# Splitting the loads of a SwiGLU kernel over two issuing queues

## Chip, cores, metric

One core of one Trainium2 chip. The engines go by their short names in the profile: ACT is ScalarE, DVE is VectorE, POOL is GpSimd and SP is SyncE; SP here only issues transfers. The metric is the device time of one execution in microseconds (us). All kernels here move the same data unless it is said otherwise. On one core a run counts as slow when it is over 1.5% above the fastest of its kernel.

## The reference

```python
x = np.random.randn(8192, 8192).astype(np.float32)

def reference(x):
    a, b = np.split(x, 2, axis=-1)
    return a * (b / (1 + np.exp(-b)))      # a * silu(b)
```

268 MB are read, 134 MB written, and there is little arithmetic per byte.

## The kernel before

Each of 32 tiles holds 256 rows of x, two per partition: a load of 8.39 MB and a store of 4.19 MB. Three buffers take turns. Silu runs in place on ACT, the multiply on DVE, and the product is stored from the same buffer, so load i+3 has to wait until store i has landed.

```python
R, BUFS = 2, 3                     # rows per partition, buffers

def load(i, rows=None):            # ... tile i is allocated at its first load
    nc.sync.dma_start(out=tiles[i][:, lo * M : hi * M], in_=xv[...])

def swiglu(i, k, c0=0, cw=half):   # row k of tile i
    nc.scalar.activation(out=b, in_=b, func=_SILU)
    nc.vector.tensor_mul(out=..., in0=a, in1=b)

def store(i, c0=0, cw=R * half):
    (nc.gpsimd if i < last - 1 else nc.sync).dma_start(out=ov[...], in_=tiles[i][...])

for i in range(BUFS):
    load(i)
for i in range(last):
    for k in range(R):
        swiglu(i, k)
    if i == last - 1:
        swiglu(last, 0)
    store(i)
    nxt = i + BUFS
    if nxt < last:
        load(nxt)
    elif nxt == last:
        load(last, (0, 1))
        load(last, (1, 2))
# ... the last tile is stored in two halves
```

## Time and profile before

| | before |
|---|---|
| time, median | 936.34 us (935.99 to 936.64, 3 runs) |
| DVE / ACT busy | 30% / 25% of the span |
| bytes moved | 402.68 MB, mean 431 GB/s over the span |
| ACT waits for loads | 687.3 us, 33 times |
| SP waits for stores | 869.5 us, 29 times |

### The profile page before, as it was taken

How to read it: one execution, taken by the hardware profiler on the slowest of the kernel's cores; microseconds unless marked ns; L12 is line 12 of the kernel's file. 1: busy time of each engine (PE TensorE's matmuls, PEld its weight loads, DVE VectorE, ACT ScalarE, POOL GpSimd, SP SyncE). 2: the span in 40 equal slices, each digit the busy share in tenths (PEclk: the TensorE clock that was granted, in tenths of full speed). 3: DMA queues.
4: the chain of work that ended last, by engine and by line, in shares of the span. 5: the costliest groups of instructions: out<-in, count | busy, mean ns of one | idle time of the engine just before them, and what ended most of it. 6: DMA issues, size and time to landing. Idle time of an engine off the chain costs nothing.

```text
span 934.3 us, 400 instructions
## 1 busy us (share of the span) xinstructions
DVE 283.3 (30%) x65; ACT 229.4 (25%) x66; POOL 16.3 (2%) x34
## 2 busy tenths in 40 slices
DVE  0333312333113332133321333213333133331252
ACT  0323330233311333113331133311333203332041
POOL 0000000000000000000000000000000000000000
DMA  9999999999999999999999999999999999999998
GB/s 404 404 449 426 425 448 424 436 429 446 428 422 441 432 446 424 446 415 453 428 421 456 415 452 421 427 450 415 442 428 441 429 435 428 438 450 414 437 432 383
DMA packets 9507, 402.68 MB, mean 431 GB/s; under 512 B 1056, under 2 KB 1056, under 8 KB 1056
## 3 DMA queue, kind: packets, MB, share of 16 engines
q1 hardware_dynamic: 5184, 276.83, 68.6%
q0 software_dynamic: 4320, 125.83, 31.2%
q14 instruction: 3, 0.02, 0.0%
HBM read 268.44 MB, written 134.22 MB: 431 GB/s over the span
## 4 chain that ended last, share of the span: by engine, by line
DMA 84%; DVE 10%; ACT 4%; issue 1%; DVEq 0%; SPq 0%; ACTq 0%
DMA out_dram<-xt 43%; DMA xt<-in_x_dram 40%; DVE xt L51 10%; ACT xt L50 4%; DVEq L106 0%; SPq L43 0%; ACTq L50 0%; DVEq L51 0%
## 5 line engine op out<-in xcount | busy, mean ns | idle before, releaser
L51 DVE TENSOR_TENSOR xt<-xt 128x4096 f32<-128x4096 f32 (+1 forms) x65 | 283.3, 4359 | 636.9 <-ACT xt L50 633.7
L50 ACT ACTIVATE xt<-xt 128x4096 f32<-128x4096 f32 (+1 forms) x65 | 228.1, 3556 | 687.3 <-DMA xt<-in_x_dram 687.3
L58 POOL DMA_DIRECT2D out_dram<-xt x30 | 16.1, 537 | 854.8 <-DVE xt L51 854.8
L50 ACT ACT_TABLE_LOAD x1 | 1.3, 1283 | 0.7 <-PEq L95 0.7
L95 POOL MEMSET const-float32-0.0<- 128x1 f32 x1 | 0.1, 99 | 0.2 <-issue 0.2
L95 POOL MEMSET const-bfloat16-1.0<- 128x1 bf16 x1 | 0.1, 102 | 0.0
L95 POOL MEMSET const-float32-1.0<- 128x1 f32 x1 | 0.1, 99 | 0.0
L95 POOL MEMSET const-uint8-127<- 128x1 uint8 x1 | 0.1, 99 | 0.0
## 6 DMA issues: line engine op xcount, KB each, us to landing
out_dram<-xt POOLq DMA_DIRECT2D x30, 4096.0 KB, 40.5
xt<-in_x_dram SPq DMA_DIRECT2D x2, 4096.0 KB, 26.4
out_dram<-xt SPq DMA_DIRECT2D x1, 4096.0 KB, 23.8
out_dram<-xt SPq DMA_DIRECT2D x2, 2048.0 KB, 14.5
xt<-in_x_dram SPq DMA_DIRECT2D x31, 33.5
```

What stands on the lines that cost most here:

```text
L50: nc.scalar.activation(out=b, in_=b, func=_SILU)
L51: nc.vector.tensor_mul(out=xt[:, k * half + c0 : k * half + c0 + cw], in0=xt[:, k * M + c0 : k * M + c0 + cw], in1=b,)
L58: (nc.gpsimd if i < last - 1 else nc.sync).dma_start(out=ov[i * P : (i + 1) * P, c0 : c0 + cw], in_=tiles[i][:, c0 : c0 + cw])
L95: nc = _bacc.Bacc("TRN2", target_bir_lowering=False, num_devices=1)
```

## The change

Its intent is to spread the issuing of loads over two queues, so that consecutive loads do not stand behind each other on SP. Stores stay as they were.

```diff
-        nc.sync.dma_start(
+        (nc.sync if i % 2 else nc.scalar).dma_start(
             out=tiles[i][:, lo * M : hi * M], in_=xv[...]
```

ACT executes its instructions in order. A load on ACT that waits for a store therefore also holds back every silu written behind it; the trace of the changed kernel below shows it, 39 us at a time.

## The prediction

> **What bounds the kernel now.** I read the page from the top: first the busy shares and the 40 slices, then the DMA queues, then the chain that ended last, and after that the list of waits and busy times of chosen stretches.
>
> ```profile
> DVE 283.3 (30%) x65; ACT 229.4 (25%) x66; POOL 16.3 (2%) x34
> ...
> DMA  9999999999999999999999999999999999999998
> ...
> q1 hardware_dynamic: 5184, 276.83, 68.6%
> q0 software_dynamic: 4320, 125.83, 31.2%
> ```
>
> The 16 DMA engines are 90% busy or more in 39 slices of 40, and the two queue rows' shares sum to 99.8% of the span. DVE and ACT work less than a third of it. So bytes bound the kernel: 402.65 MB, at this rate:
>
> ```profile
> 287.00:374.00 87.00, 26.55 (x7) 21.37 (x6) 1.60 (x3) 1.00 1.00 434
> 374.00:461.00 87.00, 26.42 (x7) 21.37 (x6) 1.60 (x3) 1.00 1.00 434
> ```
>
> These are stretches of three tiles in the steady part; the last number is GB/s. One tile is an 8.39 MB load and a 4.19 MB store, 12.58 MB, which at 434 GB/s is 29.0 us. The chain confirms it:
>
> ```profile
> 232.52 40.54 DMA out_dram<-xt
> 273.05 0.02 SPq L43
> 273.07 0.03 issue
> 273.11 33.40 DMA xt<-in_x_dram
> 306.50 0.02 issue
> 306.53 0.04 ACTq L50
> 306.56 0.04 issue
> 306.61 3.62 ACT xt L50
> ...
> 319.51 40.49 DMA out_dram<-xt
> ```
>
> Columns: start, length, what. From one store issue to that of three tiles later it is 319.51 - 232.52 = 87.0 us, 29.0 per tile. The chain looks like latency (store lands, then load, silu, multiply, store again), but with three buffers it is the queueing that fills it. A store takes 40.5 us to land although its bytes alone would need 4.19/434 = 9.7 us.
>
> From the same chain I take how two active queues share. Stores are issued 29.0 us apart and take 40.5, so each waits 11.5 us behind its predecessor and is then served for 29.0 us: 4.19/29.0 = 145 GB/s, one third. Loads take 33.5, of which 4.5 behind the predecessor, and 29.0 of service: 8.39/29.0 = 289 GB/s, two thirds. A load packet is a 64 KB row (8.39 MB over 16 engines and 8 rows each) and a store packet a 32 KB row, so one packet in turn from each queue gives just 2:1. Neither queue is ever empty. That is all that the DMA needs.
>
> **What the Trainium skill says.** (1) "DMA: Bandwidth & Descriptors", section "Queues, rings and completion order": each DMA engine goes round-robin between the queue rows that have work, a packet at a time. The 2:1 shares above agree. (2) Same page, "Issuing engines are not separate DMA queues": DMAs from scalar, sync and gpsimd run on the same 16 engines and interleave; another issuer saves only sequencer time. Here that time is small: a load's issue takes 0.328 us in the trace, and SP's wait before it is for the store, not for the sequencer. (3) Same page, "Where 436 GB/s comes from": a 435 GB/s ceiling. The measured 434 is practically at it, so nothing is left to win in the steady part. (4) Same page, "Anatomy of one DMA": a semaphore wait happens on the issuing sequencer before dispatch, and some 2.0 us per DMA are fixed. For the first the wait list below is the case's own sign (on SP). For the second, the first load is issued at 0.74 and its first packets fall into the slice 1.75 to 2.00, so 1.05 us to the first byte; the last packets start in the slice 932.0 to 932.5 and the last store lands at 920.2 + 12.9 = 933.1, about 1 us to the receipt. I take L = 2.1 us from a transfer's last byte to the first byte of the one that waited for it.
>
> ```profile
> SPq L43 <- DMA out_dram<-xt: 869.5, 29, 67.9
> ...
> ACT xt L50 <- DMA xt<-in_x_dram: 687.3, 33, 22.4
> ```
>
> **The change part by part.** Sixteen whole loads (even tiles) move from SP to ACT; SP keeps 15 whole ones and the two halves of tile 31. Bytes, transfers, packets, stores and arithmetic stay. The instruction order of the changed kernel shows on ACT: loads 0 and 2, then four silus, then one load and four silus over and over. Of ACT's loads, 14 wait for a store: load i+3 (i odd) waits for store i, and the silus of tiles i+1 and i+2 stand behind it.
>
> *Issue time:* 16 x 0.328 = 5.2 us of ACT, an engine that is idle 700 us. Off the path.
>
> *Start:* loads 0 and 1 now run side by side and both land at about 2 x 8.39/434 + 2 = 41 us, where load 0 alone landed at 22.7. Store 0 is issued near 41 + 3.6 + 2 x 4.45 = 54 instead of 35.6. But load 2 fills the DMA until then. The bytes flow on; no direct cost.
>
> *Steady state, a pair of tiles:* put store i (odd) landing at t = 0, with load i+2 (on SP) not yet finished, as the walk itself yields below.
> - t = 0: load i+3 is issued on ACT, silus of i+1 start at last (before, they ran some 25 us earlier, as soon as their tile had landed), multiplies end at about 12.6, and store i+1 is issued there. Silus of i+2 follow, store i+2 at about 22.
> - Until 13.7 only loads flow: 13.7 x 434 = 5.9 MB, of which about 1.8 finish load i+2 and 4.1 go to load i+3. Its other 4.3 MB at 289 take 14.8 us, to 28.5. Store i+1 has by then 14.8 x 145 = 2.1 MB and needs 2.05 more alone, 4.7 us: last byte at 33.2.
> - Load i+4 (SP) can flow L later, at 35.3. In these 2.1 us store i+2, already queued, has the DMA to itself: 0.9 MB. Its remaining 3.3 MB go at 145 GB/s and take 22.7 us, to 58.0. Load i+4 has by then 22.7 x 289 = 6.56 MB, and 1.83 MB are left, 4.2 us alone.
> - Store i+2 lands 1 us later: the next t = 0, with the load still in flight, as assumed. The pair took about 58 to 59 us, and twice 29.0 is 58.0.
>
> So the new wait of ACT costs nothing directly: the load left over (2L = 4.2 us of data) covers the L = 2.1 us which the next ACT load needs to start. Before, the silu could run while the store was still in flight, and other transfers covered it; now another order of transfers covers it, but with a cover of only 4.2 - 2.1 = 2.1 us, under one 64 KB packet of an engine (65.5 KB / 27.1 = 2.4 us). That is the weak point.
>
> *Mix:* per pair there are now about 14 + 7 = 21 us in which only loads or only stores flow; before there were none but at start and end. The first 2 to 35 us (loads alone) show 421 and 914 to 930 (stores alone) 421 as well, where mixed stretches show 434, so up to 3% less. Bytes are counted in lumps of 64 KB, and loads 1 and 2 landing 22 us apart speak for less loss, so I take half: 21 x 1.5% = 0.3 us per pair, 15 pairs: 5 us.
>
> ```profile
> 2.00:35.00 33.00, 8.53 (x2) 7.14 (x3) 0.00 (x0) 1.00 0.98 421
> ...
> 914.00:930.00 16.00, 4.49 (x2) 3.44 (x2) 0.00 (x0) 1.00 0.98 421
> ```
>
> *End:* load 30 is ACT's last; silus of 30 and 31 stand behind no more loads. Load 31, then stores 30 and 31, stay FIFO on SP as before, with the same stores-only tail of some 19 us. No change.
>
> Sum: 936 + 0 + 0 + 5 + 0 = 941 us.
>
> **The rivals.** *A. The new wait on ACT stalls the DMA.* For it: ACT is held until a store has landed, silus and stores bunch in pairs, and the cover is 2.1 us. If the 16 engines are apart by a packet or so, some run dry before each ACT load. A gap of 1 us per pair is 15 us (951), one of 2 us 30 us (966). Against it: the cover grows with the same delay L that has to be covered, only the slowest engine counts, and that one always has its backlog. *B. The full round trip is exposed*, with the silu, two multiplies and a store in series after the wait: 15 pairs x 12.6 = 189 us, near 1125. Against it: load i+3 itself, 19.3 us of data, is issued ahead of the silus and fills that time. *C. Two load queues are faster.* For it: the changed ring pattern, and the mostly idle ACT. Against it: 434 of 435 GB/s and 99.8% busy; the floor of the bytes is 402.65/435 = 925.6 us plus about 3 at the ends, 929, which is 0.8% below 936. It can't reach 2%. *D. Nothing at all:* no mix loss and no gap, 936.
>
> **Range and chances.** The middle lies between D and a small share of A. Downwards there is the floor of 929 and no reason to approach it: 934. Upwards, the whole 3% mix loss (10 us) and 0.6 us of gap per pair (9 us) give 955: 956. More than 2% slower begins at 955; I give that 13%, faster by 2% 1%.
>
> **What would show it right or wrong.** Right: the DMA row stays at 9 throughout; ACT's largest wait becomes a store landing ahead of its own loads, about 15 times at some 30 us; silus come in bursts of four every 58 us; loads 0 and 1 land together near 41 us; stores of odd tiles take about 37 us to land, those of even ones about 22. Wrong: DMA slices of 8 or less, GB/s near 420 and a pair clearly above 59 us would be A if the GB/s dips sit just before each ACT load, and a stronger mix effect if they lie where one kind flows alone. If shares of three active queues were by bytes and not by packets, my walk's order of landings would fail, and with it the cover.

## More of the kernel before

One more view of the kernel before is needed later, the issues of stores on POOL in order of time (start, length, engine, line, what, idle time ahead and what ended it):

```profile
145.26 0.53 POOL L58 DMA_DIRECT2D out_dram<-xt  x1 [28.97 <-DVE xt L51]
174.26 0.53 POOL L58 DMA_DIRECT2D out_dram<-xt  x1 [28.48 <-DVE xt L51]
203.54 0.53 POOL L58 DMA_DIRECT2D out_dram<-xt  x1 [28.75 <-DVE xt L51]
...
841.81 0.53 POOL L58 DMA_DIRECT2D out_dram<-xt  x1 [28.41 <-DVE xt L51]
```

Stores leave evenly, every 29 us. From 145.26 to 841.81 there are 24 tiles: 29.02 us each, 58.05 for two.

## The result

| | before | after |
|---|---|---|
| time, median of 6 runs | 935.93 us (935.80 to 936.64) | 936.73 us (936.43 to 937.55) |
| ratio after / before | | 1.0008, 95% interval 0.9995 to 1.0021 |

A ratio is the mean time of one kernel's fast runs over that of the other's fast runs of the same rounds, so not quite the ratio of the medians. The kernels take the same time.

The page of the changed kernel, first its DMA row and then its queues (packets, MB, share of 16 engines' span):

```profile
DMA  9999999999999999999999999999999999999998
...
q1 hardware_dynamic: 2880, 142.61, 35.3%
q10 hardware_dynamic: 2304, 134.22, 33.2%
q0 software_dynamic: 4320, 125.83, 31.2%
```

The loads are now on two rows, q1 (SP) and q10 (ACT), and the sum is 99.7%, against 99.8% before. The waits of ACT in the changed kernel (us in total, times, longest):

```profile
ACT xt L50 <- DMA out_dram<-xt: 547.8, 14, 40.0
ACT xt L50 <- DMA xt<-in_x_dram: 139.3, 18, 39.4
```

Before, ACT waited 687.3 us for loads alone. Now it waits 547.8 + 139.3 = 687.1 us, most of it for stores. The waiting got another name and no other length. (That the sum stays follows already from equal spans and equal work of ACT; what sets the span is the full DMA.) Two tiles of the changed kernel in order of time:

```profile
152.07 0.33 ACTq L43 DMA_DIRECT2D xt<-in_x_dram  x1
152.45 7.12 ACT L50 ACTIVATE xt<-xt 128x4096 f32<-128x4096 f32 x2 [39.30 <-DMA out_dram<-xt]
164.16 7.12 ACT L50 ACTIVATE xt<-xt 128x4096 f32<-128x4096 f32 x2 [4.59 <-DMA xt<-in_x_dram]
165.35 0.53 POOL L58 DMA_DIRECT2D out_dram<-xt  x1 [45.89 <-DVE xt L51]
177.06 0.53 POOL L58 DMA_DIRECT2D out_dram<-xt  x1 [11.18 <-DVE xt L51]
210.07 0.33 ACTq L43 DMA_DIRECT2D xt<-in_x_dram  x1
```

ACT idles 39.30 us until a store has landed, issues its load, and both silus of a tile follow. The next tile's silus wait 4.59 us for a load still in flight. Stores leave in pairs, 11.7 us apart, then nothing for 46 us. ACT's load of 152.07 has its twelfth successor at 849.10: 697.03/12 = 58.09 us per pair of tiles, against 58.05 before. Over the 12 pairs this is 0.48 us, as much as the whole 0.5 us between the two profiled spans (934.3 and 934.8), and neither can be told from noise: the 95% interval of the ratio contains 1.

Two questions were open. Where is the 5 us of the "mix" term? And is the new wait harmless because it is covered by transfers, as the prediction walked it, or because the order does not matter at all on a full DMA?

### The profile page after: what moved, and what is told of

Same layout as the page of the kernel before. It is cut to its first block, busy times and chain, and to the rows that moved or that the text cites. A ratio compares the mean times of both kernels' runs of the same rounds, so it can differ in the third digit from the quotient of the medians.

```text
span 934.8 us, 400 instructions
## 1 busy us (share of the span) xinstructions
DVE 283.2 (30%) x65; ACT 229.3 (25%) x66; POOL 16.3 (2%) x34
## 4 chain that ended last, share of the span: by engine, by line
DMA 68%; issue 24%; DVE 4%; ACT 2%; DVEq 0%; POOL 0%; SPq 0%; POOLq 0%; ACTq 0%
DMA xt<-in_x_dram 39%; DMA out_dram<-xt 30%; DVE xt L51 4%; ACT xt L50 2%; DVEq L106 0%; POOL out_dram L58 0%; SPq L43 0%; POOLq L58 0%; ACTq L43 0%; DVEq L51 0%; ACTq L50 0%
## 5 line engine op out<-in xcount | busy, mean ns | idle before, releaser
L50 ACT ACTIVATE xt<-xt 128x4096 f32<-128x4096 f32 (+1 forms) x65 | 228.0, 3555 | 687.1 <-DMA out_dram<-xt 547.8
```

## Experiments

### Rates of one kind alone (mix term)

Loads only, on SP:

```diff
-    for i in range(BUFS): ...            (the whole loop)
+    for i in range(ntiles):
+        if i >= BUFS:
+            tiles[i] = tiles[i - BUFS]
+        load(i)
+    for k in range(R):
+        swiglu(last, k)
+    store(last)
```

> Loads only, all on SP, up to three in flight, and one tile computed and stored at the end (wrong result on purpose). Measures the disputed term of the prediction: what loads alone run at. Mix-loss theory (421 GB/s when only one kind flows): tiles land 19.9 us apart, load 31 lands near 640 us, total about 668. Rival (no loss; 421 was an artefact of counting 64 KB lumps in a short stretch): 19.3 us apart, last landing near 622, total about 650.

Measured: 648.89 us (648.69 to 649.02, 4 runs). The last load landed at 622.5 us: 32 loads in 622.5 less 2.1 us of first and last latency are 19.4 us each.

The same with the changed `load`, alternating ACT and SP:

> The same loads only, alternating between ACT and SP as in the change (wrong result on purpose). If two load queues interleave at the same rate, the same time as the loads on SP alone within 0.5% (about 650 with no mix loss, 668 with it). If two queues fill gaps that one leaves, 3% faster than it; if they disturb each other, slower.

Measured: 648.89 us (648.76 to 649.10, 4 runs), the same to the hundredth. The chain of waits of this run shows SP issuing every second load (start, length, what):

```profile
194.34 0.33 SPq L43
...
233.04 0.33 SPq L43
```

233.04 - 194.34 = 38.70 us for two tiles, 16.78 MB: 433.5 GB/s. That is the rate of mixed traffic (434). Loads alone lose nothing, and two load queues are neither faster nor slower than one.

Stores only, from POOL:

```diff
+    load(0)
+    for k in range(R):
+        swiglu(0, k)
+    for i in range(ntiles):
+        store(i)                         # tile 0 each time, all on gpsimd
```

> One tile loaded and computed, then stored 32 times from the POOL queue, several in flight (wrong result on purpose). Mix-loss theory: 4.19 MB at 421 GB/s, 9.97 us per store, 319 us for the stores, about 357 in all with the 38 us ahead of the first store. Rival: 434 GB/s, 9.67 us per store, 309 and about 348 in all.

Measured: 355.21 us (355.17 to 355.40, 4 runs). Up to eight stores are in flight, and POOL may issue the next as one lands:

```profile
77.27 0.53 POOL L58 DMA_DIRECT2D out_dram<-xt  x1 [9.30 <-DMA out_dram<-xt]
...
263.92 0.53 POOL L58 DMA_DIRECT2D out_dram<-xt  x1 [9.27 <-DMA out_dram<-xt]
```

19 stores in 186.65 us are 9.82 us each, 427 GB/s, between the two theories. Stores alone do lose, but 1.6% and not 3%. With the 7 us of stores alone that the prediction counted in a pair of tiles that is 0.1 us per pair, under 2 us in all. All three kernels give wrong results on purpose.

The kept trace of the changed kernel goes further, if the packet records behind the page are read one by one and the bytes of each packet are spread over its duration. In the pair around 152.07 (149.3 to 207.3, from the last byte of one odd store to that of the next), loads flow alone for 20.9 us and stores alone for 10.0 us, together 31 us and not the 21 of the prediction; all 16 engines are busy throughout. Loads alone, from 153 to 169.5, run at 434 GB/s, stores alone, from 182 to 191.5, at 433. So in this kernel neither kind loses.

### Every load on ACT: the wait without cover

```diff
-        nc.sync.dma_start(
+        nc.scalar.dma_start(
             out=tiles[i][:, lo * M : hi * M], in_=xv[...]
```

> All 32 loads on ACT, nothing else changed. Theory (covered wait: the held-back silu costs nothing only because every second load, on SP, is still in flight when ACT's load is released): here no such load exists. Store i lands, load i+3 is issued, silu i+1 runs, store i+1 is issued 13 us later and must land before anything else is issued. Load and store together are 29.0 us of data, then 2.1 us without any transfer from the last byte to the first byte of the next load, 29 to 30 times: 936 + 62 = about 998 us; ACT waits for a store some 29 times; a dip of the DMA before each load. Rival 1 (the issuing queue does not matter at all, a saturated DMA hides any order): 936. Rival 2 (full round trip exposed, silu, multiplies and store in series after the wait): 936 + 29 x 12.6 = 1300.

Measured: 1038.90 us (1037.45 to 1040.63, 4 runs), ratio 1.1101 (1.1085 to 1.1118), correct. ACT waited for a store 29 times, as foreseen; neither rival comes near. The time lies 40 us above the theory's 998, so its size is off. A period is 428.57 - 396.05 = 32.5 us in the trace where 29.0 + 2.1 = 31.1 was expected. Busy stretches around the end of one period (the stretch and its length, busy time of DVE, ACT and POOL, clock, DMA share, GB/s; a packet counts where it starts):

```profile
425.00:426.00 1.00, 0.00 (x0) 0.00 (x0) 0.00 (x0) 1.00 1.21 524
426.00:427.00 1.00, 0.00 (x0) 0.00 (x0) 0.00 (x0) 1.00 1.21 524
427.00:428.00 1.00, 0.00 (x0) 0.00 (x0) 0.00 (x0) 1.00 0.01 0
428.00:429.00 1.00, 0.00 (x0) 0.05 (x1) 0.00 (x0) 1.00 0.00 0
429.00:430.00 1.00, 0.00 (x0) 1.00 (x1) 0.00 (x0) 1.00 2.92 983
```

No packet of data starts between 427 and 429; the first of the next load start after 429. The gap that the cover must fill is real. The packet records of this trace settle what the additional 1.4 us per tile consist of. The mean DMA engine stands empty for 59.7 us of the run, 1.7 us in the kernel before: 2.0 us for each of 29 waits, as the theory had it. The rest, 44 us, is slower packets. In every period two volleys of 16 load packets, the first after the gap and one some 3 us after the store is issued, take about 3.2 us a packet instead of 2.42. The last line above shows the first of them: 983 GB/s are 15 packets begun in that microsecond, and a DMA share of 2.92 makes them 3.1 us each. Why they are slow is not shown.

### How much slack is left: more DVE work

The first two kernels double DVE's work without touching the result. In the kernel before:

```diff
         nc.scalar.activation(out=b, in_=b, func=_SILU)
+        nc.vector.tensor_tensor(out=b, in0=b, in1=b, op=mybir.AluOpType.max)
```

> The kernel before with DVE's work doubled (each multiply preceded by a max of b with itself, 4.43 us, which leaves the result as it is). DVE is then busy 17.7 us of each 29.0, and a tile's way from load to store is 8.9 us longer. In the kernel before a buffer's round of 87 us has 11.5 us of queueing of stores and 4.5 of loads in it, more than the 8.9. Theory (transfers cover it): no change, 936 to 939. Rival (the chain of latencies is what bounds): 8.9 us per round of three tiles, 936 + 10.5 x 8.9 = 1030.

Measured: 940.83 us (937.62 to 956.33, 4 runs, the longest slow; the median of the three fast ones is 939.41); fast runs 1.0041 (1.0019 to 1.0064) of before. Practically no loss.

The same line in the changed kernel:

> The changed kernel with the same doubled DVE work. Theory (the cover has a size, and the change spent slack): after ACT's wait the first store comes 21.7 us later and the second 39.4. Load i+3 alone is through at about 20.4, so the DMA is empty 2.5 us; store i+1 lands near 33.6 and nothing else is queued, 2.1 us empty; store i+2 and load i+4 end together, 2.1 us empty again. 6.7 us per pair of tiles, 15 pairs: about 1037. Rival (DMA-bound either way, order of issue does not matter): as the kernel before with the same doubling, 936 to 939.

Measured: 1053.91 us (1053.33 to 1056.74, 4 runs), ratio 1.1267 (1.1250 to 1.1284). The DMA rows of the two, first the kernel before with doubled work, then the changed one:

```profile
DMA  9999999999999999999999999999999999999998
```

```profile
DMA  9979898898998979989989899898999889989899
```

The rival, that order does not matter, is refuted. ACT's loads in the changed kernel, one for each pair of tiles:

```profile
440.38 0.33 ACTq L43 DMA_DIRECT2D xt<-in_x_dram  x1
...
506.81 0.33 ACTq L43 DMA_DIRECT2D xt<-in_x_dram  x1
```

The pairs take 66 to 67.5 us, some 8 us more than 58, where 6.7 were worked out. So the two kernels of the same time are not equally robust: 17.7 us of DVE work per tile of 29 costs the one 0.4% and the other nearly 13%.

With half again as much DVE work, in the changed kernel and in the one before:

```diff
+        b2 = b[:, : cw // 2]
+        nc.vector.tensor_tensor(out=b2, in0=b2, in1=b2, op=mybir.AluOpType.max)
```

> The changed kernel with DVE's work half again as large (the max on half of b only, about 2.25 us more per multiply). How much slack the change has left: the second store of a pair was issued 25 us after ACT's load and the first store's last byte leaves at 35; with doubled work it comes at 39.6 and the DMA ran dry. Here it should come near 4 + 4 x 6.7 = 31, still ahead of 35, and the first store near 17.5 while the loads' data last to about 26. Threshold theory: no loss, 936 to 942. Rival (every added us of DVE work costs in proportion, half of the 117 us that the doubling cost): about 995.

> The kernel before with the same half more DVE work, for comparison: 936 to 938 by either theory.

Measured: changed 945.52 us (945.27 to 945.77), ratio 1.0103 (1.0088 to 1.0118); before 936.20 us (936.15 to 936.52), ratio 1.0004 (0.9989 to 1.0019); 4 runs each. The proportional rival (995) is out. The threshold shows in the steady part, where stores repeat every 13.3 + 44.7 = 58.0 us, without loss. The miss of 3.5 us above the range lies at the start: the first pair of stores is followed by a gap of 48.8 us instead of 44.7, and from 60 to 90 us the DMA moved 372 GB/s, against 419 in the changed kernel with normal work.

### The wait or the second queue?

In the changed kernel two things are new: ACT's wait stands ahead of the silus, and there are two load queues. This edit puts each even load behind the silus of the next tile, with doubled DVE work:

```diff
     for i in range(last):
         for k in range(R):
             swiglu(i, k)
+        if i % 2 == 0 and BUFS < i - 1 + BUFS < last:
+            load(i - 1 + BUFS)
         ...
-        if nxt < last:
+        if nxt < last and nxt % 2:
             load(nxt)
```

> The changed kernel with the doubled DVE work, but each even load is issued on ACT behind the silus of the next tile instead of ahead of them: same queues, same transfers, only the two silus before the waiting load changed places with it. Theory (it is the wait in front of the silus, not the ACT queue, that spends the slack): back to 936 to 939. Rival (two load queues, or loads on ACT at all, are the cause): near the time of the changed kernel with doubled work.

Measured: 981.05 us (979.61 to 990.97, 4 runs), ratio 1.0505 (1.0454 to 1.0556). This fits neither theory. Of the 114.5 us between 939.4 (one queue, fast runs) and 1053.9, moving the wait gives back 72.9; 41.6 remain, which the wait ahead of the silus does not explain. The same edit with normal work:

> The changed kernel with the deferred ACT loads and the normal DVE work. Both theories: 936 to 937, as the DMA is full anyway; ACT's wait for stores moves behind the silus.

Measured: 936.10 us (935.80 to 936.83, 4 runs), ratio 1.0003 (0.9986 to 1.0020), as expected. Its trace gave the clue: stores still leave unevenly, 20.6 and 37.4 us apart in turn.

```profile
412.63 0.53 POOL L58 DMA_DIRECT2D out_dram<-xt  x1 [36.81 <-DVE xt L51]
433.26 0.53 POOL L58 DMA_DIRECT2D out_dram<-xt  x1 [20.10 <-DVE xt L51]
470.68 0.53 POOL L58 DMA_DIRECT2D out_dram<-xt  x1 [36.88 <-DVE xt L51]
```

Two theories for that followed, the start, where tiles 0 and 1 land together, or the two queues in every round. One edit for each, both with the doubled DVE work:

```diff
-        (nc.sync if i % 2 else nc.scalar).dma_start(
+        (nc.sync if i % 2 or i < BUFS else nc.scalar).dma_start(   # deferred version
```

> The deferred version with doubled DVE work (981 us, its tiles landing unevenly), but the first three loads all on SP, one behind the other, so that tiles 0 and 1 no longer land together. Theory S (the start seeds the pairing): the stores come 29 us apart and the time falls to the 941 of the kernel before with doubled work. Theory Q (two load queues make it in every round: a load issued on the other queue shares the engines one to one with its predecessor instead of queueing behind it): the pairing comes back and the time stays at 970 to 985.

```diff
-        nc.sync.dma_start(
+        (nc.sync if i else nc.scalar).dma_start(                   # kernel before
```

> The reverse: the kernel before with doubled DVE work, all loads on SP but load 0 on ACT, so that tiles 0 and 1 land together as in the change and from then on there is one load queue. Theory S: the pairing of the start stays, 970 to 985. Theory Q: one queue evens the stores out to 29 us within a few rounds, 938 to 950.

Measured, 4 runs each: 981.70 us (978.35 to 983.37), ratio 1.0485 (1.0464 to 1.0506) with two queues and an even start; 947.22 us (945.50 to 950.59), ratio 1.0127 (1.0103 to 1.0152) with one queue and a paired start. Stores on POOL, first of the two-queue kernel:

```profile
523.58 0.53 POOL L59 DMA_DIRECT2D out_dram<-xt  x1 [32.33 <-DVE xt L52]
562.53 0.53 POOL L59 DMA_DIRECT2D out_dram<-xt  x1 [38.42 <-DVE xt L52]
583.77 0.53 POOL L59 DMA_DIRECT2D out_dram<-xt  x1 [20.70 <-DVE xt L52]
616.47 0.53 POOL L59 DMA_DIRECT2D out_dram<-xt  x1 [32.17 <-DVE xt L52]
```

and of the one-queue kernel:

```profile
512.79 0.53 POOL L59 DMA_DIRECT2D out_dram<-xt  x1 [28.46 <-DVE xt L52]
541.73 0.53 POOL L59 DMA_DIRECT2D out_dram<-xt  x1 [28.41 <-DVE xt L52]
570.77 0.53 POOL L59 DMA_DIRECT2D out_dram<-xt  x1 [28.51 <-DVE xt L52]
```

In the first, the gaps are 39.0, 21.2 and 32.7 us, 500 us after a start in which the tiles landed one behind the other (at 22.5, 42.1 and 69.8 us); in the second 28.9 and 29.0, though it began with gaps of 17.6, 17.6, 27.1 and 36.5. Theory S is refuted and Q stands: one first-in-first-out load queue evens the tiles out within a dozen tiles, two queues do not. One rival has to be ruled out, since in both two-queue runs ACT still waited for a store four times (116.9 us in the moved version, 105.7 us in the one with the even start). The landings in the traces do that: the tile that was held back had landed only 1.2 to 3.6 us before ACT went on, 8.5 and 6.4 us in all, and every load of both runs was issued within 0.5 us of the landing of the store that it waited for. Where the time went is the DMA: its mean engine stood empty 28.4 and 26.5 us in these two runs, against 2.7 with one queue, and slower packets as above make up the rest of their loss (16 and 20 us). The inferred reason, that a newer load takes half of the load bandwidth from the older one which is needed first, fits the shares but was not tested by itself.

No version beat the kernel before, and none was likely to: 402.65 MB at the measured 434 GB/s are 927.8 us, 0.9% under its time.

## Why the prediction was right or wrong

**What bounds the kernel, and the steady walk: right in its main course.** The DMA stayed full. ACT waited for stores 14 times (about 15 foreseen), 39 us at a time rather than 30. Loads 0 and 1 landed together at 42 us (41 foreseen). Stores of a pair left 13.3 and 25.0 us after ACT's load (12.6 and 22 foreseen) and took 22.9 and 32.9 us to land (22 and 37).

**The failed step is "Mix".** It charged 21 us per pair of tiles with a 1.5% loss, "0.3 us per pair, 15 pairs: 5 us", and this was all of the forecast's distance from 936. Loads alone run at 433.5 GB/s on one queue or two, so some 14 of the 21 us lose nothing; stores alone run at 427 by themselves and at 433 inside the changed kernel, which leaves at most 0.1 us per pair. The pairs of the changed kernel took 58.09 us against 58.05, and the whole kernel 0.8 us more; rival D, no effect at all, is what came true. The basis of the term was a misreading: 421 GB/s came from a stretch of 33 us at the very start. A packet counts whole where it starts, 16 engines then still start theirs nearly together, and one such volley of 16 x 65.5 KB is 1.05 MB. One volley more or less in 33 us is 32 GB/s, more than the 13 that were read out of it. The 421 of the stores alone, from 914 to 930, suffers in the same way: with bytes spread over the packets' durations that stretch has 432. The text named the lumps and kept half of the loss all the same. The landings of loads, 19.35 us apart over a long run, are the sound measure.

**The cover and what it had to cover were both undersized.** The walk left load i+2 with 1.8 MB to go when ACT's load is issued; the packet records show 2.7 MB at 152.07, and its last byte leaves at 161.3. But L was larger too. From the last byte of store i (149.3) to the first packet of ACT's load (155.7) it is 6.4 us, where the prediction took 2.1 from the two ends of the kernel, at which nothing else is in flight. (The "some 2.0 us" of the skill's page are a fit for transfers issued by GpSimd; the 2.1 stands on the trace alone, and the 2.0 us per wait with all loads on ACT agree with it.) So the "weak point" held, with 5.6 us in which the old load still ran beside the new one; that the two errors offset each other is luck. SP's load, too, began 4.0 us after the last byte of store i+1 (187.9 to 191.9) and not 2.1, so store i+2 had the DMA to itself for longer: 1.9 us more at 434 GB/s are 0.8 MB, which at the shared 145 GB/s would have taken 5.7 us. By this estimate it gains 3.8 us, most of the 4 between 37 and 32.9.

**Rival A was real, in other kernels.** Its stall is what all loads on ACT show (11% slower) and a part of what doubled DVE work brings out (13%, of which moving the wait gave back 72.9 of 114.5 us). In the change itself a load on SP covers it. **Rivals B and C** are out: nothing near 1125 us, and two load queues have the same rate as one.

**What the prediction did not see:** it took the second queue for neutral. For the time of this kernel it is; for the spacing of tiles, and so for the slack, it is not.

## What to carry to other kernels

When the DMA engines are full, a change of issuing queue moves waits about and leaves the time alone; ask whether any moment comes at which nothing is queued, and compute the data in flight against the latency from one transfer's end to the next one's start. Do not put a transfer that waits onto an in-order compute engine ahead of work that could run: here it cost nothing in time but used up the slack, and with doubled DVE work it accounted for 73 of the 114.5 us lost. Loads that were needed in order went best on one queue here, which kept them in order and evened them out; and rates are read from landings over many transfers, not from bytes in a short stretch.

## What the Trainium skill lacked or had wrong

- "DMA: Bandwidth & Descriptors", section "Issuing engines are not separate DMA queues", says that transfers from different engines run on the same DMA engines and interleave, and that issuing from several saves only sequencer time. For the rate the runs agree (loads alone 648.89 us on one queue and on two). It lacks that interleaving changes the order of landing: loads 0 and 1 landed together at 42 us instead of at 22.7 and 44.7, and with doubled DVE work two load queues without a wait ahead of the silus took 981 us where one queue took 939 (fast runs).
- The same page, section "Where 436 GB/s comes from", says that for transfers between HBM and SBUF the HBM side (about 358 GB/s) binds. With one core running, 434 GB/s of mixed traffic and 433.5 of loads alone were measured, close to the 435 which the section gives for the fabric; so here the fabric's figure is the one to plan with. The sentence is wrong only as it stands: a note earlier on the page, under the section "Measured", keeps about 358 to the case of both cores of a pair at work, which no run here tested.
- The same page gives no rate on trn2 for stores alone: 427 GB/s here (9.82 us per 4.19 MB) when nothing but stores ran, and 433 in the stretches of stores alone of the changed kernel.
- No page gives the time from the last byte of one transfer to the first packet of a load that waited for it while other transfers run: 6.4 us in the changed kernel (149.3 to 155.7), against 2.0 us of empty DMA where nothing else was in flight.
- That a transfer waiting on ACT holds back the activations behind it follows from two pages (ACT's queue is first-in-first-out, and the wait is on the issuing sequencer), but no page that was found draws the conclusion or gives a cost. Here it held them 39 us at a time, at no cost with other transfers in flight, and at 11% when every load was issued so.
